# One more row of the threshold search counted on ScalarE, and the equality test on VectorE

## The chip, the core and the metric

The kernel runs on one core of one Trainium2 chip. The metric is the device time of one execution in microseconds, taken as the median of several runs. The engines are TensorE (PE; its weight loads PEld), VectorE (DVE), ScalarE (ACT), GpSimd (POOL) and SyncE (SP), which here issues nearly all DMAs.

## What is computed

Two transformer layers over 1024 tokens of width 1024 in fp32. The first layer mixes a sparse attention, which looks at the 256 best keys of each query, with an RWKV-7 recurrence; both come from one projection of the normalised input. The part around the change is the choice of the keys:

```python
def block(i):                      # 128 queries from t0 = i * 128
    score = jnp.einsum('bth,bths->bts', wi, jax.nn.relu(jnp.einsum('bthd,bsd->bths', qi, ik)))
    causal = s_pos[None, :] <= t_pos[:, None]
    score = jnp.where(causal[None], score, -jnp.inf)
    _, sel = lax.top_k(score, topk)          # topk = 256
    ...
    p = jax.nn.softmax(logits, axis=-1)      # over the selected keys alone
```

## The kernel before

The kernel is written in stages. In the stage that matters here the score tiles of six query blocks are ready (`sc[2]` to `sc[7]`, 128 partitions by 384, 512, 640, 768, 896 and 1024 keys; the first two blocks have at most 256 keys and need no choice). The kernel does not sort. For every query it finds the 256th largest score bit by bit: `search` (line 859) tries one bit in a round, counts for each of the six rows of keys how many are at least the candidate, and keeps the bit where the count reaches `K`. The upper 16 bits of the scores (as int16 in `h`) are searched in 15 rounds (line 889), one further round counts the keys above the result (lines 891 and 892), the tile is reloaded with the lower 16 bits of the keys that tie (line 897), and 16 more rounds search those (line 899): 32 rounds of `counts` (line 848).

A round is: `cand` (line 863) and its negative `nv` (line 850), two operations on 128x6 on VectorE; six counts; then `pos` and `f` (lines 865 and 866), two more on 128x6 on VectorE, which need all six counts. A count on VectorE is one pass with an accumulator (line 846, written to the scratch tile `junk`). A count on ScalarE is a `Sign` activation with the bias `nv` and an accumulator (line 855, scratch tile `junka`); it returns twice the count less the length of the row, so `K` is rescaled for those rows (lines 879 and 896). The first `A` rows go to ScalarE, also for the copy that makes `h` (line 885 on ScalarE, 887 on VectorE); A is 2 before, so ScalarE counts the rows of 384 and 512.

The tail (lines 904 to 916) makes a mask for each row: the keys greater than the threshold `gt` (line 909) and their number, the keys equal to it `eq` (line 912, GpSimd before), a running count of the equal ones (line 913), the equal ones that are still needed (line 914), the sum (line 915), and on ScalarE the mask `mk` (line 916).

Written ahead of the search, and run beside it, is the RWKV projection (`Rwkv.proj`): for each of 12 columns of 128 outputs a load of 512 KB of weights (line 77), their split into two parts on ScalarE and GpSimd (lines 88 and 89), 48 matmuls (lines 105 to 107), and the token shift (`shift`): two evictions from PSUM on ScalarE (`xo`, line 1019, and `sh`, line 1021) and an add on GpSimd (line 1022). After every third column come three small products with sigmoid evictions (lines 1072 and 1080). PSUM has three buffers for these. Then eight matmuls (line 720) make a table of near biases, which ScalarE evicts (line 722) and SP writes to `nbz` (line 723). The next stage runs the attention and the recurrence together. It loads its tiles through SP (lines 1111 to 1115 for the recurrence, 962 to 966 for the attention, line 965 the near table), and the attention starts with an add of the near table and the mask on GpSimd (line 933).

The order of the instructions in each engine's queue is not written out. A planner at build time runs through a timeline by costs of its own and, on each engine, takes what is ready, that which is written earlier first. Each engine then works through its queue in that order. So ScalarE's counts stand between evictions of the projection, in an order fixed at build time, and whatever is queued behind a count that waits, waits too.

Of the kernel before, what the change touches and what calls it, by code (L numbers as in the profile page):

```python
# [8 lines left out]
FP = mybir.dt.float32  # L9
# [6 lines left out]
ALU = mybir.AluOpType  # L16
# [625 lines left out]
class Dsa:  # L642
# [187 lines left out]
    def topk(self, ap):  # L830

        c, nc = self.c, self.nc
        N, A = 6, 2
        st, sti, tk1 = self.tk
        cnt, K, sg, vs, gtc, need, pos, k1, f, cand, nv = (st[:, j] for j in range(11))
        pre, low = sti[:, 0], sti[:, 1]
# [43 lines left out]
        for j in range(N):  # L880
            x = self.sc[j + 2]
# [12 lines left out]
        for j in range(N):  # L894
            if j < A:
                nc.vector.tensor_scalar(K[:, j:j + 1], K[:, j:j + 1], -128.0 * (j + 3), None, op0=ALU.add)
            nc.vector.scalar_tensor_tensor(h[j].bitcast(U16), h[j], f[:, j:j + 1], self.sc[j + 2].bitcast(U16)[:, 0::2],
                                           op0=ALU.is_equal, op1=ALU.mult)
# [5 lines left out]
        for j in range(N):  # L904
            n = (j + 3) * 128
            x = self.sc[j + 2]
            gt = ap.tile([128, n], BF, name="gt", tag="junk", bufs=1)
            eq = ap.tile([128, n], BF, name="eq", bufs=2)
            nc.vector.scalar_tensor_tensor(gt, x, sg[:, j:j + 1], vs[:, j:j + 1].to_broadcast([128, n]), op0=ALU.mult, op1=ALU.is_gt,
                                           accum_out=gtc[:, j:j + 1])  # L910
            nc.vector.tensor_scalar(need[:, j:j + 1], gtc[:, j:j + 1], -1.0, 256.0, op0=ALU.mult, op1=ALU.add)
            nc.gpsimd.tensor_scalar(eq, x, pre.bitcast(FP)[:, j:j + 1], None, op0=ALU.is_equal)
            nc.vector.tensor_tensor_scan(x, one.to_broadcast([128, n]), eq, 0.0, op0=ALU.mult, op1=ALU.add)
            nc.vector.scalar_tensor_tensor(x, x, need[:, j:j + 1], eq, op0=ALU.is_le, op1=ALU.mult)
            nc.vector.scalar_tensor_tensor(x, x, -1.0, gt, op0=ALU.add, op1=ALU.add)
            nc.scalar.activation(self.mk[j + 2], x, AF.Copy, scale=-NEG)
# [1196 lines left out]
```

## Time and profile before

| | us |
|---|---|
| median of 3 runs | 3777.41 |
| lowest and highest run | 3772.05, 3777.46 |
| the profiled execution | 3769.52 |
| its span | 3767.8 |
| PE busy | 3326.7 (88%) |
| DVE busy | 1980.7 (53%) |
| ACT busy | 1298.1 (34%) |
| POOL busy | 1127.8 (30%) |

Busy shares are means over stages with different limits: what a change in one stage is worth is read from that stage. In a group of instructions the columns are busy time, mean duration in nanoseconds, and the idle time of the engine before them with what ended it. In a timeline the columns are start and duration in microseconds, engine, line, operation, tiles (output, arrow, inputs), shape and number; idle time before it stands in brackets with what ended it.

### The profile page before, as it was taken

What the parts mean: (1) busy time and instruction counts of PE and PEld (TensorE: products, weight loads), DVE (VectorE), ACT (ScalarE), POOL (GpSimd) and SP (SyncE); (2) the same over time, 40 slices, a digit from 0 to 9 for tenths busy, and PEclk for the clock granted to TensorE, in tenths of its full rate; (3) what the DMA queues carried; (4) which work ended last, traced back from release to release, by engine and by line L of the source; (5) the groups of instructions that cost most, each with busy time, mean ns of one, the idle gap of its engine ahead of it and who ended that gap; (6) DMA issues with size and microseconds to landing.
All of it is one profiled execution on the core that took longest, in us unless ns stands there. A gap on an engine that the chain in (4) does not pass through costs nothing. (4 is left out here: it accounts for less than half of the span.)

```text
span 3767.8 us, 42121 instructions
## 1 busy us (share of the span) xinstructions
PE 3326.7 (88%) x16048; PEld 2689.4 (71%) x16048; DVE 1980.7 (53%) x3181; ACT 1298.1 (34%) x2177; POOL 1127.8 (30%) x1007
## 2 busy tenths in 40 slices
PE   3788767898996899999998999989978899998988
PEld 2666545676774688888887788778856788876767
DVE  5569987667643412221225210026733688879983
ACT  3354433333333321111113211246633444444332
POOL 3214245434325322222223222131143222223441
PEclk7888865566567999999999999999989999998989
DMA  4552232212124321111113122210043322213244
GB/s 168 154 165 90 75 108 89 76 35 71 31 72 144 118 60 47 51 45 51 51 45 112 53 70 84 102 56 10 19 141 127 95 84 82 81 56 140 93 149 149
DMA packets 252218, 324.67 MB, mean 86 GB/s; under 512 B 16383, under 2 KB 193504, under 8 KB 250992
## 3 DMA queue, kind: packets, MB, share of 16 engines
q1 hardware_dynamic: 250960, 321.75, 26.9%
q8 instruction: 126, 2.06, 0.2%
q14 instruction: 76, 0.62, 0.1%
q0 software_dynamic: 1056, 0.23, 0.0%
HBM read 241.63 MB, written 80.29 MB: 85 GB/s over the span
## 5 line engine op out<-in xcount | busy, mean ns | idle before, releaser
L89 POOL TENSOR_TENSOR whl<-wraw,whl 128x1024 fp32r<-128x1024 f32 (+1 forms) x128 | 286.6, 2244 | 882.5 <-ACT whl L88 879.2
L105 PE MATMUL ps<-h,whl 128*128 128x512 f32 x1216 | 477.8, 395 | 17.7 <-ACT h L214 13.6
L106 PE MATMUL ps<-h,whl 128*128 128x512 f32 x1216 | 478.5, 394 | 3.5 <-POOL h L215 3.5
L107 PE MATMUL ps<-h,whl 128*128 128x512 f32 x1216 | 477.1, 392 | 0.0
L105 PEld LDWEIGHTS ps<-h,whl 128*128 128x128 f32 x1216 | 230.9, 190 | 69.3 <-ACT h L214 15.9
L88 ACT ACTIVATE whl<-wraw 128x1024 fp32r<-128x1024 f32 (+1 forms) x128 | 125.2, 988 | 440.8 <-issue 225.0
L106 PEld LDWEIGHTS ps<-h,whl 128*128 128x128 f32 x1216 | 231.1, 190 | 54.4 <-POOL h L215 6.4
L107 PEld LDWEIGHTS ps<-h,whl 128*128 128x128 f32 x1216 | 231.0, 190 | 48.4
L532 DVE TENSOR_TENSOR silu<-silu,ps 128x1024 f32<-128x1024 f32 x22 | 26.9, 1221 | 431.8 <-PE ps L107 431.8
L288 PE MATMUL ps<-h,op 128*128 128x512 f32 x616 | 237.4, 391 | 6.1 <-ACT op L311 5.2
L289 PE MATMUL ps<-h,op 128*128 128x512 f32 x616 | 240.4, 390 | 0.0
L290 PE MATMUL ps<-h,op 128*128 128x512 f32 x616 | 239.9, 390 | 0.0
L597 PE MATMUL o<-pT,v 128*128 128x256 f32 (+1 forms) x640 | 156.7, 364 | 13.7 <-ACT pT L592 7.7
L313 POOL TENSOR_TENSOR op<-t,op 128x512 fp32r<-128x512 f32 x44 | 73.3, 1666 | 305.1 <-ACT op L311 268.9
L592 ACT ACTIVATE pT<-tp 128x512 fp32r<-128x512 f32 (+2 forms) x221 | 94.6, 444 | 186.7 <-PE tp L589 149.9
L1388 DVE SCALAR_TENSOR_TENSOR cv<-up,v_fw,cv 128x1023 f32<-128x1023 f32 x88 | 134.1, 1524 | 30.0 <-ACT cv L1386 29.8
L105 PE MATMUL ps<-wo,h 128*128 128x512 f32 x320 | 128.9, 412 | 18.9 <-ACT wo L1398 16.5
L288 PE MATMUL ps<-op,op 128*128 128x512 f32 x308 | 123.9, 405 | 24.1 <-ACT op L412 14.9
L106 PE MATMUL ps<-wo,h 128*128 128x512 f32 x320 | 129.8, 411 | 15.1 <-POOL wo L1399 15.1
L597 PEld LDWEIGHTS o<-pT,v 128*128 128x128 f32 x640 | 116.8, 238 | 36.4 <-ACT pT L592 14.0
L846 DVE TENSOR_SCALAR_CACHE_REDUCE junk<-h,tk 128x640 bf16<-128x640 int16 (+7 forms) x128 | 137.9, 1077 | 3.4
L288 PEld LDWEIGHTS ps<-h,op 128*128 128x128 f32 x616 | 116.2, 189 | 30.9 <-ACT op L311 5.6
(593 smaller groups left out, 8118.1 us busy)
## 6 DMA issues: line engine op xcount, KB each, us to landing
wraw<-in_w_ffn_up_dram SPq DMA_DIRECT2D x66, 512.0 KB, 3.9
adaw<-in_ada_w_dram SPq DMA_DIRECT2D x96, 256.0 KB, 3.4
wraw<-in_w_in_dram SPq DMA_DIRECT2D x42, 512.0 KB, 4.0
wraw<-in_w_ffn_gate_dram SPq DMA_DIRECT2D x22, 512.0 KB, 3.9
wraw<-in_w_ffn_down_dram SPq DMA_DIRECT2D x22, 512.0 KB, 3.6
f_d<-cv SPq DMA_DIRECT2D x22, 512.0 KB, 2.6
raw<-in_w_ffn_down_dram SPq DMA_DIRECT2D x22, 512.0 KB, 7.7
raw<-f_d SPq DMA_DIRECT2D x22, 512.0 KB, 5.5
```

Source lines behind the costliest of these rows:

```text
L88: self.nc.scalar.activation(hl[:, 0], raw, AF.Copy)
L89: self.nc.gpsimd.tensor_sub(hl[:, 1], raw, hl[:, 0].bitcast(FP))
L105: self.nc.tensor.matmul(out, lh, rh, start=first and i == 0, stop=False)
L106: self.nc.tensor.matmul(out, lh, rl, start=False, stop=False)
L107: self.nc.tensor.matmul(out, ll, rh, start=False, stop=last and i == n - 1)
L288: mm(out, lh, rh, start=start and i == 0, stop=False, skip_group_check=True)
L289: mm(out, lh, rl, start=False, stop=False, skip_group_check=True)
L290: mm(out, ll, rh, start=False, stop=stop and i == n - 1, skip_group_check=True)
L592: nc.scalar.activation(pT[:, 0, 0:n, q], x, AF.Copy)
L597: nc.tensor.matmul(o[:, q], v[:, b0 + s].rearrange("p a d -> p (a d)"), pT[:, x, s, q], start=b0 == 0 and n == 0, stop=end and n == 3)
L846: nc.vector.tensor_scalar(junk, x, thr, None, op0=ALU.is_ge, op1=ALU.add, accum_out=out)
L1388: nc.vector.scalar_tensor_tensor(out[:, s:], ps[:, :T - s], w[2 - s][:, j:j + 1], out[:, s:], op0=ALU.mult, op1=ALU.add)
```

## The change

The constant A goes from 2 to 3: in each of the 32 rounds ScalarE counts the row of 640 keys as well, VectorE the remaining three; the copy that makes `h[2]` moves to ScalarE, and `K` of that row gets the two rescalings (lines 879 and 896), two short operations more on VectorE. And the test for equals in the tail moves from GpSimd to VectorE, six instructions.

```diff
-        N, A = 6, 2
+        N, A = 6, 3
...
-            nc.gpsimd.tensor_scalar(eq, x, pre.bitcast(FP)[:, j:j + 1], None, op0=ALU.is_equal)
+            nc.vector.tensor_scalar(eq, x, pre.bitcast(FP)[:, j:j + 1], None, op0=ALU.is_equal)
```

## Rows read from the trace of the kernel before

**Rows 1.** Head of the page.
```profile
span 3767.8 us, 42121 instructions
```
**Rows 2.** By stretch: busy PE, PEld, DVE, ACT, POOL (instructions); clock, DMA share, GB/s.
```profile
307.50:516.00 208.50, 165.14 (x621) 124.67 (x619) 198.31 (x392) 96.23 (x179) 65.43 (x32) 0.82 0.22 75
516.00:550.00 34.00, 18.31 (x32) 8.84 (x31) 32.69 (x44) 12.49 (x19) 25.48 (x20) 0.53 0.29 110
550.00:570.00 20.00, 3.30 (x14) 2.95 (x15) 4.94 (x14) 4.73 (x11) 5.71 (x10) 0.50 0.90 254
```
**Rows 3.** Groups of VectorE instructions from 303 to 550 us.
```profile
L846 DVE TENSOR_SCALAR_CACHE_REDUCE junk<-h,tk 128x640 bf16<-128x640 int16 x16 | 14.0, 872 | 0.0
L846 DVE DVE_READ_ACCUMULATOR junk<-h,tk 128x1 f32 x128 | 10.5, 82 | 0.0
L850 DVE TENSOR_SCALAR tk<-tk 128x6 f32<-128x6 f32 x31 | 5.3, 170 | 1.0
L865 DVE TENSOR_TENSOR tk<-tk 128x6 f32<-128x6 f32 x31 | 18.1, 584 | 3.3
L866 DVE SCALAR_TENSOR_TENSOR tk<-tk 128x6 f32<-128x6 f32 x31 | 22.3, 719 | 1.5 <-DVE tk L865 0.5
```
**Rows 4.** Groups of ScalarE instructions from 303 to 550 us.
```profile
L1019 ACT ACTIVATE xo<-ps,mu 128x1024 f32<-128x1024 f32 x12 | 13.2, 1098 | 3.0 <-PE ps L107 3.0
L855 ACT ACTIVATION_READ_ACCUMULATOR junka<-h,tk 128x1 f32 x64 | 11.9, 187 | 0.0
L855 ACT ACTIVATE junka<-h,tk 128x512 bf16<-128x512 uint16 x16 | 11.5, 720 | 0.5
L855 ACT ACTIVATE junka<-h,tk 128x384 bf16<-128x384 uint16 x16 | 9.8, 615 | 55.1 <-DVE tk L850 55.1
```
**Rows 5.** Timeline: an undisturbed round, and a short operation beside GpSimd's add.
```profile
371.80 0.62 ACT L855 ACTIVATE junka<-h,tk 128x384 bf16<-128x384 int16 x1 [3.68 <-DVE tk L850]
377.03 0.61 ACT L855 ACTIVATE junka<-h,tk 128x384 bf16<-128x384 int16 x1 [3.68 <-DVE tk L850]
...
508.35 2.39 POOL L1022 TENSOR_TENSOR xo<-xo,sh 128x1023 f32<-128x1023 f32 x1 [9.60 <-ACT sh L1021]
509.08 1.69 DVE L865 TENSOR_TENSOR tk<-tk 128x6 f32<-128x6 f32 x1
```
**Rows 6.** Waits from 303 to 550 us: total, times, longest.
```profile
ACT junka L855 <- DVE tk L850: 105.0, 30, 7.3
PE ps L105 <- ACT sh L1021: 47.6, 6, 17.7
```
**Rows 7.** Groups of VectorE instructions from 303 to 550 us: the tail.
```profile
L914 DVE SCALAR_TENSOR_TENSOR scb<-scb,tk,eq 128x640 f32<-128x640 f32 x1 | 2.8, 2802 | 0.0
L909 DVE SCALAR_TENSOR_TENSOR gt<-scb,tk 128x896 bf16<-128x896 f32 x1 | 1.9, 1886 | 0.0
L914 DVE SCALAR_TENSOR_TENSOR scb<-scb,tk,eq 128x1024 f32<-128x1024 f32 x1 | 1.3, 1286 | 0.0
L882 DVE TENSOR_SCALAR scb<-scb,tk 128x1024 f32<-128x1024 f32 x1 | 0.7, 749 | 0.0
```
**Rows 8.** Timeline from the end of the search to the first add of the attention.
```profile
520.84 1.10 ACT L1019 ACTIVATE xo<-ps,mu 128x1024 f32<-128x1024 f32 x1
533.11 11.76 SPq L723 DMA_DIRECT2D nbz<-nbt  x7
549.53 1.06 ACT L916 ACTIVATE mk<-scb 128x1024 bf16<-128x1024 f32 x1 [5.00 <-DVE scb L915]
550.61 0.37 SPq L1111 DMA_DIRECT2D sg<-sg_d  x1
566.93 1.68 POOL L933 TENSOR_TENSOR nb<-near,mk 128x128 f32<-128x128 f32 x3 [10.60 <-DMA near<-nbz]
```
**Rows 9.** Line 965, the load of the near table, four in the kernel.
```profile
DMA to landing us min/median/max: 2.6/3.2/11.3
```
**Rows 10.** Busy time by stretch, columns as in rows 2.
```profile
600.00:1100.00 500.00, 446.40 (x2977) 344.76 (x2976) 332.82 (x857) 170.32 (x378) 201.51 (x320) 0.59 0.20 57
```

## The prediction

> **What bounds the kernel now.** I read the page first: one core, a span of 3767.8 us [rows 1]. Then the busy time by stretch, around the code that changes. From 307.5 to 516 us VectorE is busy for 198.3 of 208.5 us, ScalarE for 96.2, GpSimd for 65.4; the tail of the same function, 516 to 550 us, has VectorE busy for 32.7 of 34 us [rows 2]. The reader is to see that one engine is full there and that the others have room. Next the view of what waited for what: ScalarE stood 105.0 us in 30 waits for VectorE's line 850, and TensorE 47.6 us for evictions (line 1021) that lie in ScalarE's queue behind those waits [rows 6]. So the threshold search on VectorE sets the pace of the RWKV projection too.
>
> Last the timeline, for what this stage releases. ScalarE writes the last mask from 549.53 to 550.59 us, and SP, which waited for ScalarE, issues the first load of the next stage at 550.61 us [rows 8]. The twenty microseconds behind it carry a burst of loads (DMA share 0.90, TensorE busy 3.3 us) [rows 2], and attention begins at 566.93 us, when the table of near biases has landed [rows 8]. A microsecond taken from the search can therefore reach the end of the kernel, as long as nothing else becomes late in its place. The stage behind, 600 to 1100 us, has TensorE busy for 446.4 of 500 us at a mean granted clock of 0.59 [rows 10]: it has little idle time in which a delay or a gain at its start could vanish, so I take its start as shifting its end.
>
> **The search.** Each of 32 rounds (15, 1 and 16) has four counts on VectorE and two on ScalarE, then four short operations on VectorE. A round that nothing disturbs takes 5.23 us: two ScalarE counts that wait for line 850 start at 371.80 and 377.03 us [rows 5]. The change takes the 640-element count away: 0.872 + 0.082 = 0.95 us [rows 3], and 32 of them are 30.5 us. One correction of K more in each of two places and the first copy of the third row, now on ScalarE, are single short operations in 240 us and cost nothing that can be seen.
>
> What replaces it: ScalarE counts 384 elements in 0.615 and 512 in 0.720 us, so 640 at about 0.825 us, an estimate from these two; with three accumulator reads of 0.187 us the three counts take 2.7 us [rows 4]. VectorE's round becomes 5.23 - 0.95 = 4.28 us, of which four short operations (0.17 us each, line 850's mean [rows 3]) are 0.7, so its counts end some 3.6 us into the round. ScalarE has 0.9 us to spare. But it also evicts the projection: for each of 11 columns in the search an xo (1.098 us [rows 4]), an sh and a weight rounding of about the same length, 3.2 us together. Behind the three counts these mostly fit (2.7 + 3.2 = 5.9 against a round of 4.3, with 0.9 to spare in the next one); between two counts they make VectorE wait 3.2 - 0.9 = 2.3 us. Bounds: 0, and 11 x 2.3 = 25 us. I take +4, nearer to the lower end, because most columns stand behind both counts in ScalarE's queue before.
>
> The Trainium skill speaks against this part: "ScalarE: Activation LUTs", Rules for kernel authors, sends simple operations to VectorE, which it puts at up to three times the speed. The rows do not bear it out for a count with an accumulator, 0.95 us there against about 1.01 us on ScalarE [rows 3, 4]; by the page a count that moves would lengthen its engine's work threefold, by the rows it changes engine at equal price.
>
> There is also a cost that I expect to shrink. The short operations of lines 865 and 866 average 0.584 and 0.719 us where line 850, of the same shape, takes 0.170: 31 x (0.414 + 0.549) = 30 us [rows 3]. One case shows the cause: GpSimd adds from 508.35 to 510.74, and line 865, started at 509.08, lasts 1.69 us, to 510.77 [rows 5]. That is 2.7 us for each of 11 columns. The order in each queue is fixed by a planner that lays out the projection by time; with rounds shorter by 0.95/5.23 = 18%, about 9 columns instead of 11 fall into the search. I take -5 us; bounds -15 (adds that now fall under counts) and +10 (more short operations that meet an add).
>
> Search: -30.5 + 4 - 5 = -31.5 us, so it ends at about 484.5 instead of 516 us; bounds -45 and +4.
>
> **The tail.** Six tests for equals move from GpSimd to VectorE. Their form is that of line 882, at 0.749 us for 1024 elements [rows 7]; six rows of 384 to 1024, 4224 elements, give 3.1 us by size, and I take 3.5 for the fixed part of the short ones. In return line 909 is no longer slowed by the test beside it: 1.886 us at 896 elements, where line 914, also a pass over two inputs, takes 1.286 at 1024 with no test beside it [rows 7], so 1.13 by size; 0.75 us too much, and about 2.6 over the five rows that had a test beside them. Net +0.9 us. No wait on GpSimd is left in the tail, and GpSimd, some 15 us freer, adds the projection's rows sooner. Upper bound: a test held behind an add as line 914 was (2.802 us at 640 elements [rows 7]), three columns at about 2.4 us, +8. Lower bound 0. The threshold chain then ends at 550.6 - 31.5 + 0.9 = 520 us.
>
> The Trainium skill ("SBUF — State Buffer", Who interferes with whom) calls the port that VectorE shares with GpSimd an exclusive lock. Line 914's 2.802 us agrees; line 909 beside a test was slowed by 0.75 us and not held, which is not the page's full block. By the page each moved test could stand behind an add, the +8 above; by the line 909 row, none.
>
> **What is late next.** The table of near biases comes from matmuls that TensorE runs behind the projection. Before, the last of its eight writes goes out when SP's run of seven ends at 533.11 + 11.76 = 544.87 us [rows 8], 29 us behind the end of the search and hidden by the tail. If two more columns are left over at the end of the search, this chain gets longer. From below: both columns lie finished in PSUM and only their evictions remain, 2 x 2.2 = 4.4 us: 484.5 + 29 + 4.4 = 518 us. From above: the last column's eviction stands behind the last mask in ScalarE's queue, as it stands behind the first one before (520.84 us [rows 8]): 520 + 24 = 544 us. I take 535, nearer to the upper one, which is the order seen. The load of the table then comes behind the burst and lands in about 3 us, not 11.3 [rows 9], after a write for which I take the 2.6 us of the fastest load: 541 us where it was 566.9. That is -26 us, less than the -31 of the threshold chain, so it is the later of the two. Other vectors that pass the same queues behind it I put at 2 us. Forecast: -24 us.
>
> SP, the DMAs and GpSimd's own queue get no new instruction; GpSimd loses six.
>
> **Rivals.** *All of it arrives* (-38 us): ScalarE's foreign work falls behind the counts, GpSimd's adds fall under counts (-30.5 - 8), and the table is written by 518 us. For it: ScalarE idles 112 of 208 us [rows 2]. Against it: the order of the queues. Time 3739. *The projection eats it* (about -3): half of the left-over columns is computed after the search at the low clock (0.53 in the tail before [rows 2]), and their evictions wait for masks; the table lands at about 564 us. Time 3774. *ScalarE ends each round*: its foreign work lies between the counts of nearly every column (+25) and the search keeps its length but for 5 us. Time 3772. *Slower*: the planner lays out the next stage anew, and TensorE gets less of its clock there. Its 446.4 busy us at 0.59 become 484 at 0.544, +38, and 38 - 24 = +14; it decides from 0.56 on, where the loss is the whole 24 us. For it: that stage already runs near the lower of TensorE's two levels, 1.2 and 2.4 GHz. Against it: nothing in the change touches it. Time 3791.
>
> **How the numbers follow.** The profiled execution took 3769.5 us, 1.7 us around its span; the runs have a median of 3777.4, 0.2% more. The forecast is 3745.5 by the profiled one and 3777.4 - 24 = 3753.4 us by the median, own range 3744 to 3762. Chances: forecast 0.46, all of it 0.22, eaten 0.18, ScalarE 0.03, slower 0.11. A measurement here can tell about 0.2%, 7.6 us. Faster by more: 0.46 + 0.22 + 0.02 of eaten = 0.70; within: 0.16 + 0.03 = 0.19; slower: 0.11. The range 3738 to 3778 leaves out slower (0.11), the far end of all of it (0.05) and of eaten (0.04).
>
> **What would show it.** Right: undisturbed rounds of about 4.3 us; 32 x 3 counts on line 846 and as many on line 855; the search over by about 485 us; the last mask near 520 us; attention's first GpSimd add near 541 us, and a later stage of unchanged length. Wrong: VectorE idle before line 865 for more than some 10 us in all (ScalarE late); lines 865 and 866 at means as high as before or higher; more than two columns left over; the near table later than 550 us; or a stage from 600 to 1100 us that grows by more than it started early.

## The result, and the profile after

The changed kernel took 3723.06 us (median of 4 runs, 3718.92 to 3737.76) where the kernel before took 3774.73 in the same comparison: a ratio of 0.9871, 95% interval 0.9851 to 0.9890. Two later comparisons gave 3736.45 (0.9909, 0.9886 to 0.9933) and 3738.40 (0.9904, 0.9881 to 0.9928). All 12 runs of the changed kernel have a median of 3735.5 us. The kernel before has one of 3773.6 over the 82 runs of these and two further comparisons (3773.9 with the ten of a run of its own, d_before); between 3773.6 and 3735.5 the gain is 38 us. The forecast was 24 us. Single runs of the kernel before lie between 3757 and 3791 us, so what follows goes by medians and by stretches of the trace that repeat. Much of this spread goes with TensorE's granted clock, whose mean over the execution is on record for each run. Through 88 runs of the kernel before the time falls by some 2.4 us for each 0.001 of it (an estimate, a straight line). In the first comparison three of the four runs of the changed kernel had 0.887 to 0.889 and took 3719 to 3723 us; its other nine had 0.880 to 0.885 and took 3727 to 3742. The 52 us of the first comparison are in part a lucky clock.

The head of the page of the slowest of the first four runs (3737.8 us), and the busy time by stretch (busy PE, PEld, DVE, ACT, POOL; clock, DMA share, GB/s): the search, the tail, the 20 us behind it, and 600 to 1100 us.

```profile
span 3736.0 us, 42098 instructions
```
```profile
307.50:495.30 187.80, 157.93 (x612) 119.84 (x612) 154.77 (x325) 125.05 (x243) 65.37 (x32) 0.87 0.25 83
495.30:528.50 33.20, 17.60 (x31) 8.38 (x31) 32.50 (x50) 11.15 (x19) 13.60 (x17) 0.52 0.41 138
528.50:548.50 20.00, 8.46 (x29) 6.49 (x29) 8.85 (x28) 8.05 (x16) 6.94 (x9) 0.50 0.84 266
600.00:1100.00 500.00, 451.62 (x3009) 353.96 (x3009) 329.36 (x852) 172.25 (x384) 198.58 (x310) 0.59 0.19 55
```

Against [rows 2] VectorE's share of the search falls from 95% to 82%, and ScalarE's rises from 46% to 67%: VectorE now stands idle at times. Where it waits is in the groups of VectorE (303 to 550 us; busy time, mean ns, idle time ahead and what ended it) and in the view of the waits (total, times, longest).

```profile
L865 DVE TENSOR_TENSOR tk<-tk 128x6 f32<-128x6 f32 x31 | 17.6, 568 | 27.7 <-ACT junka L855 25.6
L866 DVE SCALAR_TENSOR_TENSOR tk<-tk 128x6 f32<-128x6 f32 x31 | 11.5, 372 | 1.1
L846 DVE DVE_READ_ACCUMULATOR junk<-h,tk 128x1 f32 x96 | 7.9, 82 | 0.0
L850 DVE TENSOR_SCALAR tk<-tk 128x6 f32<-128x6 f32 x31 | 5.5, 177 | 1.0
```
```profile
ACT junka L855 <- DVE tk L850: 48.0, 23, 3.7
PE ps L105 <- ACT sh L1021: 25.9, 4, 9.6
DVE tk L865 <- ACT junka L855: 25.6, 11, 5.7
```

The group of 640 elements on line 846 [rows 3] is gone and 32 of its accumulator reads with it. ScalarE waits 48.0 us for VectorE instead of 105.0 [rows 6]. New is the last line: eleven times VectorE stands at line 865, up to 5.7 us, for ScalarE's counts; before it stood there for 3.3 us in all [rows 3]. ScalarE's timeline shows one case: the evictions of a projection column stand between its second and its third count.

```profile
431.12 0.61 ACT L855 ACTIVATE junka<-h,tk 128x384 bf16<-128x384 uint16 x1 [1.80 <-DVE tk L850]
431.87 0.72 ACT L855 ACTIVATE junka<-h,tk 128x512 bf16<-128x512 uint16 x1
432.59 1.10 ACT L1019 ACTIVATE xo<-ps,mu 128x1024 f32<-128x1024 f32 x1
433.59 1.10 ACT L1021 ACTIVATE sh<-ps,v_c 128x1023 f32<-128x1023 f32 x1
434.58 1.05 ACT L88 ACTIVATE whl<-wraw 128x1024 fp32r<-128x1024 f32 x1
435.53 0.82 ACT L855 ACTIVATE junka<-h,tk 128x640 bf16<-128x640 uint16 x1
```

Behind the search, SP's queue, the last masks and the first add of the attention, in order of time:

```profile
515.17 0.32 SPq L723 DMA_DIRECT2D nbz<-nbt  x1
523.66 1.27 SPq L962 DMA_DIRECT2D kHL<-k_d  x2
528.49 1.06 ACT L916 ACTIVATE mk<-scb 128x1024 bf16<-128x1024 f32 x1 [5.23 <-DVE scb L915]
529.57 0.38 SPq L1111 DMA_DIRECT2D sg<-sg_d  x1
532.62 0.37 SPq L965 DMA_DIRECT2D near<-nbz  x1
539.27 1.68 POOL L933 TENSOR_TENSOR nb<-near,mk 128x128 f32<-128x128 f32 x3 [3.96 <-DMA near<-nbz]
```

The last mask ends at 529.55 us (550.59 before [rows 8]), the attention begins at 539.27 (566.93). Between the two lie 10 us, not 16, because the planner now puts the two loads of line 962 ahead of the load that waits for the last mask. The last write of the table of near biases goes out by 515.5 us and lands at 518.3, well before it is wanted; what the attention waits for is the table's load, which stands in SP's queue behind the load that waits for the mask.

### The profile page after: what moved, and what is told of

It reads as the page before. It is cut to its first block, busy times and chain, and to the rows that moved or that the text cites. A ratio compares the mean times of both kernels' runs of the same rounds, so it can differ in the third digit from the quotient of the medians.

```text
span 3736.0 us, 42098 instructions
## 1 busy us (share of the span) xinstructions
PE 3325.1 (89%) x16048; PEld 2691.6 (72%) x16048; DVE 1939.7 (52%) x3124; ACT 1327.3 (36%) x2242; POOL 1116.4 (30%) x1001
## 5 line engine op out<-in xcount | busy, mean ns | idle before, releaser
L105 PE MATMUL ps<-whl,fT 128*128 128x512 f32 x352 | 137.5, 391 | 0.3
```

Source lines behind the costliest of these rows:

```text
L105: self.nc.tensor.matmul(out, lh, rh, start=first and i == 0, stop=False)
```

## Where the time went

For each kernel one profiled execution (three of the changed one, two of the one before) gives: the search, from the first line 882 to the first use of its result (line 900); the wait from the start of line 916's last mask to the first line 933; the start of the attention; and the length of the stage of attention and recurrence, from there to the last line 945. The time is the median of its runs, the clock the mean over its runs of TensorE's granted clock in the whole execution. The last column is the change of the time less the change of the start, against 3773.6 and 566.0 us: what the later stages did beyond following their start. The intervals of the ratios leave the times open by some 5 to 9 us either way, and the start is that of one execution, so an entry of less than some 9 us in the last column is not told from nothing. In the changed kernel a part of the higher mean lies in the search itself, where 0.88 was granted against 0.82 and 0.84 before; that part brings the later stages nothing. The kernels are those of the experiments below.

| kernel | search | wait for loads | attention starts | stage behind | time | clock | beyond the start |
|---|---|---|---|---|---|---|---|
| before | 213.9, 213.0 | 17.4, 16.5 | 566.9, 565.1 | 596.5, 599.6 | 3773.6 | 0.879 | 0 |
| changed | 194.9, 194.8, 194.9 | 10.8, 10.6, 11.5 | 539.3, 541.7, 540.3 | 597.6, 587.4, 578.6 | 3735.5 | 0.883 | -12.5 |
| b_count3 | 195.1 | 10.2 | 541.2 | 597.2 | 3746.9 | 0.880 | -1.9 |
| c_eq | 213.0 | 10.7 | 555.7 | 586.1 | 3759.2 | 0.881 | -4.1 |
| j_rep1 | 203.9 | 11.0 | 549.6 | 590.1 | 3747.1 | 0.882 | -10.1 |
| o_rep3 | 212.9 | 10.5 | 556.5 | 594.4 | 3757.8 | 0.883 | -6.3 |
| i_rep6 | 225.0 | 10.5 | 565.7 | 583.1 | 3774.7 | 0.875 | +1.4 |
| p_brep1 | 219.1 | 18.0 | 572.0 | 601.6 | 3779.5 | 0.878 | -0.1 |
| m_bar_before | 213.4 | 18.1 | 564.5 | 605.9 | 3768.3 | 0.880 | -3.8 |
| n_bar_after | 194.9 | 16.5 | 540.2 | 610.9 | 3746.3 | 0.883 | -1.5 |
| x_12 | 189.5 | 30.6 | 560.9 | 585.1 | 3749.2 | 0.885 | -19.3 |
| g_a4 | 220.5 | 11.3 | 564.0 | 593.3 | 3768.2 | 0.880 | -3.4 |
| f_psum | 190.9 | 10.5 | 534.3 | 592.6 | 3756.5 | 0.881 | +14.6 |
| k_nonv | 185.4 | 23.3 | 543.4 | 582.1 | 3734.2 | 0.885 | -16.8 |
| l_nonv_psum | 174.3 | 10.6 | 520.1 | 604.1 | 3731.4 | 0.882 | +3.7 |

For the changed kernel the sum is: search -18.6, tail 0, wait for loads -6, and a search that began 1 us earlier, together the attention 25.6 us earlier (the means of three and two executions); and 12.5 us more from behind it. In all nine kernels whose two loads of line 962 stand ahead of the wait for the last mask, the wait for loads is 10.2 to 11.5 us; where line 1111 comes first it is 16.5 us or more.

## The experiments

My theory after the result: the time follows the start of the attention one to one, the start is as forecast, and the rest of the gain comes from stages that the planner lays out anew. Rival one: one half of the change does something in the later stages by itself. Rival two: the later stages are shorter because they start earlier. Rival three: the rest is the difference between executions.

**The change again, and its halves.**

> The changed kernel once more, for a second trace and its spread. Its search ended 20.9 us earlier than before (495.3 against 516.2 us) and its attention began 27.6 us earlier (539.3 against 566.9 us), yet the median of its runs is 51.7 us lower (3723.1 against 3774.7). Theory 1 (a steady gain of the planner's new order behind the search): every trace of this kernel shows a later stage shortened by some 15 to 20 us against the kernel before. Theory 2 (the executions of one kernel differ by 15 us): the stages differ between two traces of this same kernel, 3718 to 3738 us, and the steady gain is about the 28 to 32 us of the first trace.

> The changed kernel a third time, beside the experiments on the same chip. Two traces of it so far agree to 1 us up to the start of the attention's length of waits (search 194.9 and 194.8 us after its first sign multiplication, tail 33.2, loads 10.8 and 10.6) and differ in the stage of attention and recurrence: 597.6 against 587.4 us, with a granted clock of 0.58 against 0.65 in its fifth hundred microseconds. If that is chance of the execution, this trace lies anywhere from 585 to 600 us there, and the median is 3719 to 3740 us. If the order of the changed kernel shortens that stage, all its traces lie below the 596.5 and 599.6 us of the kernel before.

> The kernel before once more, for a second trace and for what a comparison of equal kernels shows: 3765 to 3778 us, ratio within 0.3% of 1. Theory 2 expects its traces to differ from each other in the same stages in which the traces of the changed kernel differ.

> The third row counted on ScalarE alone, the test for equals left on GpSimd. If the gain is the search's, nearly all of it is here: search over near 495 us, total within 8 us of the changed kernel (3715 to 3735 us). If moving the test brings a good part, this one stays at 3740 to 3755 us.

> The test for equals on VectorE alone, two rows counted on ScalarE. By the prediction's tail the threshold chain gets 0.9 us longer: 3770 to 3780 us, no change. If the freed GpSimd or a new order of SP's loads is worth something by itself, 3745 to 3765 us.

```diff
b_count3:
-        N, A = 6, 2
+        N, A = 6, 3
c_eq:
-            nc.gpsimd.tensor_scalar(eq, x, pre.bitcast(FP)[:, j:j + 1], None, op0=ALU.is_equal)
+            nc.vector.tensor_scalar(eq, x, pre.bitcast(FP)[:, j:j + 1], None, op0=ALU.is_equal)
```

Measured: the changed kernel 3736.45 and 3738.40 us, the kernel before 3776.21 (ratio 1.0000, 0.9982 to 1.0017), the count alone 3746.86 (0.9938, 0.9917 to 0.9959), the test alone 3759.22 (0.9961, 0.9948 to 0.9974). The count alone has the whole gain of the search (195.1 us) and the earlier loads; its time follows its start to within 2 us, and lies where I had put it if moving the test brings a good part. The test alone moves neither search (213.0) nor tail (32.9 against 33.3 us), and still the kernel is 14 us faster, where the prediction's tail would have made it 0.9 slower: its attention starts 10 us earlier, 6 of them because here too the loads of line 962 stand ahead of the wait, 3 because its search began earlier. So an edit that saves nothing on its own engine gained through the order that it made the planner lay out. Neither half shows anything beyond its start that the intervals tell from nothing: rival one is not borne out. And the count alone starts its attention at 541.2 us, with the same order of loads as the changed kernel, without the 12.5 us: an early start and early loads are not enough for them. The stage of attention and recurrence, in the three executions of the changed kernel and the two of before (columns as above):

```profile
539.30:1136.90 597.60, 530.99 (x3495) 413.64 (x3495) 389.36 (x1019) 209.10 (x466) 239.19 (x360) 0.60 0.20 58
```
```profile
541.70:1129.10 587.40, 520.34 (x3495) 405.15 (x3495) 389.46 (x1019) 209.36 (x466) 239.67 (x360) 0.62 0.21 59
```
```profile
540.30:1118.90 578.60, 511.43 (x3495) 399.61 (x3495) 388.37 (x1019) 208.79 (x466) 239.31 (x360) 0.63 0.21 60
```
```profile
566.90:1163.40 596.50, 524.10 (x3496) 405.73 (x3495) 389.74 (x1019) 208.54 (x466) 237.60 (x360) 0.61 0.20 58
```
```profile
565.10:1164.70 599.60, 528.69 (x3495) 409.57 (x3495) 390.09 (x1018) 208.94 (x466) 237.88 (x360) 0.61 0.20 58
```

One program, the same 3495 matmuls, and the stage is 597.6, 587.4 and 578.6 us long: TensorE's busy time, 531.0 to 511.4, goes with the granted clock, 0.60 to 0.63. That is rival three at work, 19 us between executions; the executions as a whole lie 10 us apart (3737.8, 3732.4 and 3727.3), so about half of it is given back elsewhere. What is left without TensorE's busy time repeats: 66.6, 67.1 and 67.2 us against 72.4 and 70.9. Of the 12.5 us, then, some 4.7 are time in this stage in which TensorE is not busy; the next stage, up to the first line 532, gives 4 more (181.9 and 181.7 us before, 177.4, 176.1 and 180.7 after); the rest is TensorE's busy time, which goes with the granted clock. That the new order closes those gaps is not shown: j_rep1 has 74 us without TensorE's busy time and 10 us beyond its start.

**Does the time follow the start?**

> The changed kernel with the six counts done twice in the first six rounds of the second search (the second counting writes the same numbers). A round of counts without three of its short operations is about 4.31 - 3 x 0.17 = 3.8 us, so the search should last 194.9 + 6 x 3.8 = 218 us, a little longer than before (213.5), and attention should start at 563 to 565 us, where it did before. If the later stages only follow their start, the time is that of before, about 3770 to 3776 us. If the later stages of the changed kernel are shorter for a reason of their own, whatever their start, it is 3737 + 23 = about 3760 us. If it is the order that the planner happens to lay out, the stage of attention and recurrence and the one behind it come out at lengths of their own again, anywhere within some 15 us of these.

> The changed kernel with the six counts done twice in one round only: +3.8 us in the search, attention starts 4 us later. One to one: 3737 + 4 = 3741 us, the stage of attention and recurrence 588 us long and the one behind it 177, as in the changed kernel. If the order of the later stages is laid out by chance, a shift of 4 us is enough to move these two lengths and the time by more than 8 us in either direction.

> The changed kernel with the counts done twice in three rounds: by the runs with one and six (203.9 and 225.0 us) the search should last 212 us and attention start at 556 to 557 us, 10 us ahead of before. One to one with the start of before: 3764 us. If the changed kernel keeps some 11 us beyond its start, as it does with one repeated round: 3753. If what is kept shrinks with the shift, in between.

> The kernel before with the counts done twice in one round: the search 5 to 9 us longer, attention starts at 571 to 575 us. One to one: 3779 to 3783 us. If the lengths of the later stages are laid out anew with every shift, by chance, it can come out 10 us to either side of that, even faster than before.

```diff
                 counts(view)
+                if bits == 16 and b >= 10:      # 15 in j_rep1 and p_brep1, 13 in o_rep3
+                    counts(view)
```

Measured: i_rep6 3774.73 (1.0002, 0.9983 to 1.0020), j_rep1 3747.08 (0.9933, 0.9915 to 0.9951), o_rep3 3757.76 (0.9943, 0.9922 to 0.9965), p_brep1 3779.45 (1.0008, 0.9994 to 1.0021). One repeated round cost 9 us of search instead of 3.8, six cost 30 instead of 23: ScalarE's late counts come again in the repeated ones (VectorE idle before the comparison for 30.9 us with one and 30.7 with six by the view of the waits, in the changed kernel 25.6). The kernel before, shifted by 6 us, goes one to one. With the attention back at 565.7 us i_rep6 takes the time of before, and from the changed kernel to six repeats the time grows by 39 us for 25 us of later start, with one and three in between. That looks like rival two, an extra that melts away as the start goes back, but the clock is a rival that these runs don't leave out. The twelve runs of i_rep6 have the lowest clock of all kernels, 0.875 (0.868 to 0.881), where the kernel before has 0.879 in the same comparison; at 2.4 us for each 0.001 (the estimate above) this is some 10 us. Its search doesn't explain it: the clock there is 0.83 in its trace, 0.82 and 0.84 before. At the clock of before it would take about 3765 us, nearer to the 3760 of a gain that stays whatever the start than to 3774; its profiled run, at 0.881, took 3761. So whether the extra melts is not shown, and neither is why this kernel is granted less clock.

**The boundary taken away.**

> The kernel before with a barrier over all engines behind the threshold search: no load and no work of the stage of attention and recurrence may start until the last mask and the table of near biases are done. Beside the run with the same barrier in the changed kernel it shows what the search alone is worth when both stages behind start from the same state. By itself I expect it 2 to 15 us slower than before, since some loads and small steps of that stage can no longer run ahead.

> The changed kernel with the same barrier. The search and tail are 18.7 us shorter in it (194.9 + 33.2 against 213.5 + 33.3). If the gain beyond the earlier start comes from what the planner lets run ahead of the last mask (the loads that go out 10 us earlier, their order), the barrier takes it away and the difference between the two runs with a barrier is 17 to 21 us. If the stage of attention and recurrence is shorter in the changed kernel for another reason, the difference stays at 30 us or more.

```diff
                     d.topk(tk)
+        tc.strict_bb_all_engine_barrier()
```

Measured: 3768.28 (0.9984, 0.9970 to 0.9998) and 3746.31 (0.9916, 0.9901 to 0.9932), 22 us apart by the medians and 26 by the ratios. Their attentions start 24.3 us apart (564.5 and 540.2), with the same order of loads in both (line 1111 first, wait 18.1 and 16.5 us). So without anything that runs ahead of the last mask the gain fits the earlier start. The two intervals leave the 26 us open by some 8 either way: the 37 that an extra of 12.5 would make lie outside, the 21 of my theory and the 30 of the rival inside. The profiled markers say why the difference is more than the search: this execution also began its search 3.8 us earlier. My forecast for the kernel before with the barrier, 2 to 15 us slower, was wrong: it is 5 us faster by the median. The extra may therefore hang on what crosses the boundary between the two stages; the early loads alone don't carry it, since b_count3 has them too. What does stays open.

**A late near table.**

> The kernel before with 12 rounds instead of 16 in the second search: the last four bits of the threshold are left out, nothing of the change is in it. Its search gets 4 x 5.23 = 21 us shorter, as it did by the change, with the same work per round on every engine. If a microsecond taken from the search is a microsecond at the end, the total falls by 21 to 28 us (the latter with the shorter wait for loads seen in the changed kernels): 3745 to 3755 us. If an earlier end of the search brings more in the stages behind, as the changed kernel's 35 to 50 us suggest, it falls by 35 us or more: below 3740 us.

```diff
-        search(lambda j: h[j].bitcast(U16), 16)
+        search(lambda j: h[j].bitcast(U16), 12)
```

Measured: 3749.18 (0.9936, 0.9916 to 0.9957), 24 us below before, by as much as the search is shorter, but the trace shows another way than I had in mind. SP's queue, the last mask and the first add of the attention, and below them its stage of attention and recurrence:

```profile
530.27 1.06 ACT L916 ACTIVATE mk<-scb 128x1024 bf16<-128x1024 f32 x1 [3.26 <-DVE scb L915]
534.95 0.40 SPq L1111 DMA_DIRECT2D sg<-sg_d  x1
549.85 0.85 SPq L723 DMA_DIRECT2D nbz<-nbt  x2
555.41 0.37 SPq L965 DMA_DIRECT2D near<-nbz  x1
560.92 2.11 POOL L933 TENSOR_TENSOR nb<-near,mk 128x128 f32<-128x128 f32 x3 [3.89 <-DMA near<-nbz]
```
```profile
560.90:1146.00 585.10, 505.32 (x3484) 394.51 (x3483) 391.02 (x1018) 207.72 (x465) 233.18 (x358) 0.64 0.20 57
```

The last mask came 19 us earlier (530.3), the near table was late, as my forecast had feared for the change, and the attention began 30.6 us behind the mask, only 5 us earlier than before. The time fell by 24 us all the same. One reading is that it followed the last mask, which releases the loads of the recurrence (line 1111), and not the attention's first add. The kernel k_nonv (below) has the recurrence's loads ahead as well; its SP queue and the first add:

```profile
521.17 0.38 SPq L1111 DMA_DIRECT2D sg<-sg_d  x1
528.44 0.70 SPq L962 DMA_DIRECT2D kHL<-k_d  x1
531.76 0.36 SPq L965 DMA_DIRECT2D near<-nbz  x1
```
```profile
543.38 1.67 POOL L933 TENSOR_TENSOR nb<-near,mk 128x128 f32<-128x128 f32 x3 [9.13 <-DMA near<-nbz]
```

The recurrence's loads go out at 521 us, the near table's 10 us behind them; the attention starts 3 us later than in the changed kernel, and the kernel is not slower by its median. But these two kernels have the highest clocks of the table, x_12 0.885 (0.884 to 0.887) against 0.879 before, and in their stage of attention and recurrence 0.64 where before has 0.61. By the estimate of 2.4 us for each 0.001 some 15 of the 24 us of x_12 go with that, and 9 are left for a mask that is 19 us and an attention that is 5 us earlier. So these runs don't decide which of the two the end follows, nor whether the late attention is what raised the clock.

**A fourth row on ScalarE.**

> Four rows counted on ScalarE, two on VectorE, the test on VectorE. ScalarE's four counts take 0.61 + 0.72 + 0.83 + 0.94 + 4 x 0.19 = 3.9 us a round, VectorE's two 2.6 us. If ScalarE's lateness is what took back part of the gain, VectorE now waits for it in nearly every round: about 32 x 4.6 us plus the foreign evictions, search 195 to 215 us after the first sign multiplication instead of 194.9, total 3735 to 3765 us. If ScalarE's evictions fit beside its counts, the search falls by another 30 us: 3700 to 3715 us.

```diff
-        N, A = 6, 3
+        N, A = 6, 4
```

Measured: 3768.15 (0.9998, 0.9983 to 1.0012). The groups and the waits of VectorE:

```profile
L865 DVE TENSOR_TENSOR tk<-tk 128x6 f32<-128x6 f32 x31 | 14.1, 456 | 93.6 <-ACT junka L855 93.6
L866 DVE SCALAR_TENSOR_TENSOR tk<-tk 128x6 f32<-128x6 f32 x31 | 5.2, 166 | 1.1
```
```profile
DVE tk L865 <- ACT junka L855: 93.6, 31, 8.8
```

All 31 rounds end with ScalarE now, where it was 11; the search is 220.5 us, longer than before and longer than the 195 to 215 expected, and the time lies above the expected 3735 to 3765 us. Of two, three and four rows three has the shortest search, and at three the rival "ScalarE ends each round" already held for a third of the rounds.

**What holds the short operations up.**

> The changed kernel with the search's K and f in PSUM, so that lines 865 and 866 read one input from SBUF and one from PSUM (one short copy more). If GpSimd's adds hold those two operations because both read two inputs from SBUF, their means fall from 0.568 and 0.372 us to about 0.17 us and the search gets up to 18 us shorter; part of it can come back as waiting for ScalarE's counts, 25.6 us now: total 3705 to 3730 us. If something else holds them, means and total stay (3720 to 3740 us).

> The changed kernel without line 850: the candidate is kept half below the integer, VectorE counts the keys that are less, ScalarE takes the sign of candidate minus key, and no negative of the candidate is needed. It takes 32 x 0.177 = 5.7 us of short operations out of the rounds; the GpSimd adds that stand in the way remain. If VectorE ends most rounds, the search lasts 189 to 190 us and the time falls by 5 us to about 3732; if ScalarE ends the disturbed ones anyway, by 3 to 4 us.

> The same with K and f in PSUM, so that each of the three short operations left in a round has one operand there. If what GpSimd's adds hold up is short operations with all operands in SBUF (the 0.52 us mean of line 852 in the run with K and f in PSUM), none is left, all three should take 0.16 to 0.18 us, and the search loses up to 18 us more, less what ScalarE's late counts keep: 175 to 186 us, attention from 520 to 531 us. Passed on one to one this is 3718 to 3729 us. If the hold-up moves on to the counts themselves, the search stays at 188 us or more. If the PSUM buffer costs later stages what the earlier run with it seemed to lose (18 us), it is 3736 to 3750.

```diff
l_nonv_psum (f_psum alike):
+        kf = c.psum([128, 2, 6], "kf")
+        K, f = kf[:, 0], kf[:, 1]
k_nonv and l_nonv_psum:
-            nc.vector.tensor_scalar(nv, cand, -1.0, 0.5, op0=ALU.mult, op1=ALU.add)
...
-                    nc.scalar.activation(junk, x, AF.Sign, bias=nv[:, j:j + 1], accum_out=cnt[:, j:j + 1])
+                    nc.scalar.activation(junk, x, AF.Sign, bias=cand[:, j:j + 1], scale=-1.0, accum_out=cnt[:, j:j + 1])
...
-            nc.vector.memset(f, 0.0)
+            nc.vector.memset(f, -0.5)
```

Measured: f_psum 3756.45 (0.9957, 0.9932 to 0.9982), k_nonv 3734.23 (0.9899, 0.9879 to 0.9919), l_nonv_psum 3731.39 (0.9892, 0.9868 to 0.9916). The groups of f_psum (its lines stand two further down: 865, 867 and 868 are 863, 865 and 866, and 852 is 850), then of l_nonv_psum (one further down, without line 850):

```profile
L852 DVE TENSOR_SCALAR tk<-tk 128x6 f32<-128x6 f32 x32 | 16.6, 519 | 1.1
L868 DVE SCALAR_TENSOR_TENSOR kf<-tk,kf 128x6 f32<-128x6 f32 x31 | 5.3, 170 | 1.1
L865 DVE TENSOR_SCALAR tk<-kf 128x6 f32<-128x6 f32 x31 | 5.1, 164 | 1.1
L867 DVE TENSOR_TENSOR tk<-tk,kf 128x6 f32<-128x6 f32 x31 | 5.0, 161 | 32.2 <-ACT junka L857 30.4
```
```profile
L867 DVE SCALAR_TENSOR_TENSOR kf<-tk,kf 128x6 f32<-128x6 f32 x31 | 5.3, 170 | 1.3 <-DVE tk L866 0.2
L864 DVE TENSOR_SCALAR tk<-kf 128x6 f32<-128x6 f32 x31 | 5.1, 164 | 1.1
L866 DVE TENSOR_TENSOR tk<-tk,kf 128x6 f32<-128x6 f32 x31 | 5.0, 161 | 27.7 <-ACT junka L856 25.8
```

With one operand in PSUM the comparison falls from 568 to 161 ns and the update from 372 to 170. In f_psum the hold-up moved to the next operation with all operands in SBUF, line 850, whose mean had been 170 and 177 ns: 519 ns. With that one gone as well, nothing of the round is held up, and the search takes 174.3 us, just below the 175 expected; without line 850 alone (k_nonv) it takes 185.4. Single instructions show the same. Before, ten operations of line 865 and nine of line 866 took over 0.3 us, and each of these ended within 0.15 us of the end of a GpSimd operation. In f_psum 11 or 12 of each of the three operations with an operand in PSUM ran wholly beside a GpSimd operation, and none took over 0.17 us. One case:

```profile
371.45 2.39 POOL L89 TENSOR_TENSOR whl<-wraw,whl 128x1024 fp32r<-128x1024 f32 x1
372.32 0.16 DVE L867 TENSOR_TENSOR tk<-tk,kf 128x6 f32<-128x6 f32 x1 [2.64 <-ACT junka L857]
372.52 0.17 DVE L868 SCALAR_TENSOR_TENSOR kf<-tk,kf 128x6 f32<-128x6 f32 x1
372.73 0.17 DVE L865 TENSOR_SCALAR tk<-kf 128x6 f32<-128x6 f32 x1
```

A count of 1024 elements takes 1.28 us beside one or not. So GpSimd's adds hold up VectorE's short operations that work in SBUF alone, with one input or two, and neither those with an operand in PSUM nor the counts. The Trainium skill ("SBUF — State Buffer", Who interferes with whom) has it so: an exclusive port, for two inputs in SBUF and for a one-input `tensor_scalar` in its two-port mode, and not for the form that writes an accumulator. These traces agree.

For the time it was worth little. l_nonv_psum starts the attention 20 us ahead of the changed kernel and ends 4 us ahead by the median, which the intervals don't tell from nothing: TensorE was busy for 537.7 us of a stage of 604.1. Its 3731.4 us lie between the two forecasts, 3718 to 3729 passed on one to one and 3736 to 3750. f_psum, for which I had expected 3705 to 3730 us and a search up to 18 us shorter (4 came), starts 6 us ahead and ends 21 us behind, with 198.4 us between the last line 945 and the first line 532 where the changed kernel has 176 to 181. No version clearly beats the changed kernel.

## Why the prediction was wrong, point by point

**The time.** 3753.4 us forecast, 3723.1 measured (3735.5 over all runs), below the range of 3738 to 3778.

**The count moved at equal price: right.** An undisturbed round takes 4.31 us (counts of line 855 at 426.81 and 431.12), 4.28 forecast; the 640-count on ScalarE 0.827 us, 0.825 forecast.

**ScalarE late, +4: mis-sized.** VectorE's idle time before line 865 went from 3.3 to 27.7 us, +24.4, at my upper bound of 25. The price was right: 25.6 us in eleven waits are 2.3 us each, as worked out. The number of columns that pay it was wrong. I read the order of before, where columns stood behind both counts, as the order after; the planner put columns between the second and the third count. I had named 10 us of idle time there as the sign that this step was wrong.

**GpSimd's adds, -5: mis-sized.** The excess of lines 865 and 866 over line 850 fell from 29.9 to 31 x (0.391 + 0.195) = 18.2 us, -11.7, within the bounds. The reason given for the -5, fewer columns inside the search, did not come: thirteen adds of line 1022 start in the search before and thirteen after. They fall elsewhere in the rounds now; line 866 is held three times instead of nine (over 0.3 us), line 865 twelve times instead of ten. Sum of the search: -30.5 + 24.4 - 11.7 = -17.8; measured -18.6 (means). Forecast -31.5.

**The tail, +0.9: right.** 33.2 us instead of 33.3. The six tests take 5.6 us, of which one stood behind an add (2.64 us at 512 elements); the masks of line 909 fell by 2.6 us together, as worked out, and the held line 914 from 2.80 to 0.89.

**The near table later of two: wrong.** Its last write was to go out at about 535 us, in fact it did at 515.5. I had columns left over at the end of the search; none was. The last `sh` eviction of the projection (line 1021) starts at 494.9 us, inside the search, where before it started at 521.8, behind it. I had also not seen that the order of SP's queue was free to change: the wait for loads shrank by 6 us in every kernel in which line 962 went ahead. The start, 541 forecast and 540.4 measured, came out right by luck: the search gained 13 us less than forecast, and from the end of the last mask to the attention it took 10 us where the forecast had 21 (520 to 541). The two errors cancel.

**The start shifts the end, later stages unchanged: the step that failed.** "I take its start as shifting its end" put the stages behind at nothing, and the start did come as forecast; the stages behind gave 12.5 us more. The rival for which the planner lays out the next stage anew was in the text, but only with a loss. Runs with other edits show what lies beyond the start at anything from -19 to +15 us, and within 4 us of nothing in the two with a barrier between the stages. Of the 12.5 us some 8.5 stand in the means of three executions outside TensorE's busy time or in the next stage, the rest in busy time that goes with the granted clock. What brings them stays open: neither half of the change alone shows any of it clear of the noise, and an early start with early loads (b_count3) is not enough. "All of it arrives" (3739) was the number nearest to the result, and not its way: that rival has the search 38.5 us shorter, and 18.6 came.

## What to carry to other kernels

A planner's order is part of every edit: an edit that saves nothing where it stands moved this kernel by 14 us, 6 of them through the order of the loads. A forecast should therefore carry a term of both signs for the stages behind, here some 15 us, beside the sum for the edit itself. And when work moves to an engine with foreign work in its queue, count that work as lying in the way between the moved pieces unless the order of the new kernel is known.

## What was not expected of the hardware

The same program's stage of attention and recurrence took 578.6 to 597.6 us with TensorE busy for 511 to 531 us at a granted clock of 0.63 to 0.60: a single profiled execution can't show a gain of 10 us there. Over many runs the mean clock is nevertheless a mark of the kernel: the runs of the kernel before average 0.879 in each of four comparisons, while kernels that differ from it in the search and its tail alone average 0.875 (i_rep6) to 0.885 (x_12). What an edit does to the clock of later stages is then worth 10 us and more, and no run here shows what decides it. And a short VectorE operation with a single SBUF input, at a mean of 0.17 to 0.19 us in the kernels that kept K and f in SBUF, took 0.52 us once it became the first of its round to work in SBUF alone beside GpSimd's adds.
